# A hybrid decoder layer: another order in which heads, gates and parts of x are admitted

## The chip, the cores and the metric

The kernel runs on one core of one Trainium2 chip. The metric is the device time of one launch in microseconds (us). A time that is given without more is the median of several runs of the same program. The profile is that of one single execution.

## What is computed

One layer of a decoder over a prompt of 2,048 tokens and 8 sample tokens. The input is normalised and multiplied by one wide matrix `w_in` (1,024 x 11,280). Its columns feed two branches and two merge gates: a gated DeltaNet with 8 heads (GDN, a recurrence over chunks of tokens), and a dilated window attention with 3 groups of 4 heads.

```python
def mixer_inputs(x, g_pre, w_in):
    xn = rms_norm(x, g_pre)
    proj = jnp.einsum('bld,de->ble', xn, w_in)
...
    def step(S, inp):
        u_c, w_c, qk_c, qd_c, kd_c, gl_c = inp
        v_new = u_c - jnp.einsum('bhcd,bhde->bhce', w_c, S)
        o_c = jnp.einsum('bhcd,bhde->bhce', qd_c, S) + jnp.einsum('bhce,bhef->bhcf', qk_c, v_new)
        S = S * gl_c[..., None, None] + jnp.einsum('bhcd,bhce->bhde', kd_c, v_new)
        return S, o_c
...
def merge_residual(x, p_a, p_b, gate_a, gate_b, w_out, g_post):
    h = jax.nn.sigmoid(gate_a) * p_a + jax.nn.sigmoid(gate_b) * p_b
    out = jnp.einsum('bld,de->ble', h, w_out)
    return x + rms_norm(out, g_post)
```

The sample tokens go through the same layer, with a GDN state and key and value caches that are read from memory. All states are outputs too.

## The kernel before

**Two halves.** The prompt is worked on in two halves of 1,024 tokens (`hf` 0 and 1); the sample tokens ride with the first. For each half the input projection runs over 128-column tiles of `w_in`, two tiles at a time. After both halves a final phase multiplies by `w_proj_a`, `w_proj_b` and `w_out` in four token groups.

**Products (`main`).** A pair of tiles is one call of `step`. It saves multiplications on half of the contraction by sums of inputs and weights. Its products read `xs1k` to `xs7k` and `xp4s` to `xp7s` (x, transposed) against `wh` and `wl` (the weights, split into a high and a low part); in a row of TensorE a product has one of these names, and `bank0` to `bank3` as its target. The order inside a pair is fixed: product 1, product 7, product 6, product 2 and so on. Product 6 (`xs6k`) accumulates onto a copy of product 1 in `bank1`, so it waits (`at_b`) until `bank1` has been emptied by the `sink` of the pair before.

**Pages and tokens.** A `sink` copies a finished tile from its PSUM bank into a page `pg` (17 pages of SBUF, 4 KB a partition and a little more) and then frees the bank. The first of a tile's sinks waits for `t.admit`, the tile's token, and then for a free page. Tokens (17, as many as pages) are given out by `admitter` strictly in the order of the list `admits`; a request that can't be met holds up all that stand behind it. A task hands its tokens back when it is done with its pages. So when tokens run out, the sinks stop, the banks stay full, and `main` stops before a product.

**Side tasks.** On `bank4` to `bank7` run the heads. `gdn` of a head does a convolution, transposes, a triangular inverse, and then a serial loop over 8 chunks, each a chain through three engines: kT times `st` on TensorE, `rr` on VectorE (L311), U times `rr` on TensorE, a copy to `ww` (ScalarE L280 or VectorE L355), kd times `ww` on TensorE, `st` on VectorE (L311). TensorE rows that read `st`, `rr` or `ww` are this loop. One head is in the loop at a time. `attn` is the attention of a group and head, `combine` joins the groups, `sample_gdn` and `sample_attn` are the sample tokens, `prep` loads, normalises and transposes x for a half and forms the sums of its rows on VectorE (L316 on pages).

**What sets the order.** All of these are generators. `Scheduler.run` plays them at build time with a table of costs and latencies and writes each engine's instruction list in the order in which it finds them ready, ties going by priority. On the chip each engine runs its list in that order, and a wait at the head of the list holds all behind it.

**`ORDER`.** Two strings (L2171 and L2172), one for each half, are read a character at a time. `G` adds the three tiles of the next GDN head (and claims 4 more tokens for its work), `Z` that head's gate tile, `a` the q, k and v tiles of one attention group (each fourth `a` is a combine gate), `g` a merge gate tile. `x` and `y` claim 5 and 4 tokens for the preparation of the second half's x, `S`, `T` and `C` claim 4, 3 and 1 for the sample GDN, the sample attention and the convolution state. The string thus sets both the order of the tiles in the projection (`p["work"]`) and the order of `admits`. Lines of the trace: all matmuls are L251, transposes L267, ScalarE L280, VectorE L299, L301, L311, L316 and L355, loads and stores L400.

Of the kernel before, what the change touches and what calls it, by code (L numbers as in the profile page):

```python
# [453 lines left out]
def build(nc, tc, ctx, I, O):  # L454
# [1702 lines left out]
    def conv_state():  # L2157
# [10 lines left out]
    plan, admits = [], []  # L2168


    ORDER = ("GZaaGaZaGaagZGgaZagGZaagGagagZGagaZGaZagggggggxgyg",  # L2171
             "gGgZggaagGaZSagGaZaGaZgaggGaagTZGaZaCggGaaZgGZaggag")  # L2172
    for hf in range(2):
        tiles = []

# [45 lines left out]

        for what in ORDER[hf]:
            if what in "GZag":
# [108 lines left out]
def trace(nc, arrays):  # L2332
    from contextlib import ExitStack

    ins = {n: nc.dram_tensor(f"in_{n}", a.shape, mybir.dt.from_np(a.dtype), kind="ExternalInput").ap()
           for n, a in arrays.items()}
    outs = [nc.dram_tensor(f"out_{i}", s, F32, kind="ExternalOutput").ap() for i, s in enumerate(_OUTS)]
    with tile.TileContext(nc) as tc, ExitStack() as ctx:
        return build(nc, tc, ctx, ins, outs)
# [13 lines left out]
```

## Time and profile before

| | |
|---|---|
| median of 3 runs | 3048.79 us (3048.49 to 3049.93) |
| the profiled execution | 3050.04 us |
| its span in the trace | 3048.2 us |
| TensorE busy | 3010.0 us, 99% of the span |
| TensorE weight loads busy | 2692.0 us, 88% |
| VectorE, ScalarE, GpSimd busy | 72%, 40%, 5% |
| mean granted TensorE clock | 0.996 |

The profiled execution lies 1.25 us above the median, and 1.84 us of its time are outside the span. Times inside the trace count from the start of the span. TensorE is called PE in the rows, its weight loads PEld, VectorE DVE, ScalarE ACT. A granted clock of 1.00 is 2.4 GHz, one of 0.5 is 1.2 GHz. The ends of matmuls are modelled in the trace and overlap the next matmul, so how long a matmul holds the engine is read from start to start.

### The profile page before, as it was taken

How to read it: one execution, taken by the hardware profiler on the slowest of the kernel's cores; microseconds unless marked ns; L12 is line 12 of the kernel's file. 1: busy time of each engine (PE TensorE's matmuls, PEld its weight loads, DVE VectorE, ACT ScalarE, POOL GpSimd, SP SyncE). 2: the span in 40 equal slices, each digit the busy share in tenths (PEclk: the TensorE clock that was granted, in tenths of full speed). 3: DMA queues.
4: the chain of work that ended last, by engine and by line, in shares of the span. 5: the costliest groups of instructions: out<-in, count | busy, mean ns of one | idle time of the engine just before them, and what ended most of it. 6: DMA issues, size and time to landing. Idle time of an engine off the chain costs nothing.

```text
span 3048.2 us, 55885 instructions
## 1 busy us (share of the span) xinstructions
PE 3010.0 (99%) x20879; PEld 2692.0 (88%) x20879; DVE 2199.2 (72%) x5978; ACT 1212.9 (40%) x3444; POOL 141.1 (5%) x239
## 2 busy tenths in 40 slices
PE   7999999999999999999999999999999999999999
PEld 7999999999999999978887888888888888897887
DVE  6777767786778686767586868597988486666765
ACT  5545444344435443433442534343434343313121
POOL 1000000000000000000000000000000000000000
PEclk9999999999999999999999999999999999999999
DMA  4323242332233325332244332336452236565463
GB/s 125 94 73 89 58 112 71 99 85 83 70 98 89 89 79 147 110 85 81 73 121 124 88 88 80 105 96 186 137 158 86 76 100 180 176 204 197 149 226 117
DMA packets 468760, 343.46 MB, mean 113 GB/s; under 512 B 88745, under 2 KB 411825, under 8 KB 468480
## 3 DMA queue, kind: packets, MB, share of 16 engines
q1 hardware_dynamic: 468488, 339.89, 38.1%
q8 instruction: 164, 2.69, 0.4%
q14 instruction: 108, 0.88, 0.1%
HBM read 261.40 MB, written 80.97 MB: 112 GB/s over the span
## 4 chain that ended last, share of the span: by engine, by line
PE 94%; DVE 3%; DMA 2%; ACT 1%; issue 0%; SPq 0%; POOL 0%; DVEq 0%; POOLq 0%; ACTq 0%
PE bank L251 89%; PE bank L267 5%; DVE pg L311 1%; DMA wr<-in_w_in 0%; DVE wl L316 0%; DVE pg L316 0%; SPq L400 0%; DMA pg<-in_cache_v_w 0%; DMA pg<-in_x_prompt 0%; DMA pg<-in_state_gdn 0%; DMA pg<-gate 0%; ACT L280 0%; DMA ghh<-in_g_head_norm 0%; DVE wh L355 0%; DVE junk L311 0%
## 5 line engine op out<-in xcount | busy, mean ns | idle before, releaser
L280 ACT ACTIVATE pg<-bank 128x256 f32<-128x256 f32 (+7 forms) x741 | 331.8, 460 | 759.4 <-PE bank L251 690.0
L316 DVE TENSOR_TENSOR wl<-wr,wh 128x512 fp32r<-128x512 f32 x595 | 383.5, 647 | 21.3 <-ACT wh L280 3.3
L355 DVE CAST wh<-wr 128x512 fp32r<-128x512 f32 (+1 forms) x384 | 153.0, 399 | 206.9 <-PE bank L251 184.0
L251 PE MATMUL bank<-xp7s,wh 128*128 128x512 f32 (+3 forms) x1196 | 302.1, 328 | 0.0
L251 PE MATMUL bank<-xp6s,wh 128*128 128x512 f32 (+3 forms) x1132 | 290.1, 330 | 0.0
L251 PE MATMUL bank<-xp5s,wh 128*128 128x256 f32 (+3 forms) x1100 | 276.3, 327 | 0.0
L280 ACT ACTIVATE wh<-wr 128x512 fp32r<-128x512 f32 (+1 forms) x213 | 129.8, 611 | 351.9 <-PE bank L251 292.1
L251 PE MATMUL bank<-xp4s,wh 128*128 128x260 f32 (+2 forms) x1068 | 267.5, 326 | 1.6 <-DVE xp4s L311 1.6
L316 DVE TENSOR_TENSOR bank<-bank,etmp 128x256 f32<-128x256 f32 (+2 forms) x260 | 134.9, 519 | 129.4 <-PE bank L251 126.3
L251 PEld LDWEIGHTS bank<-xp7s,wh 128*128 128x128 f32 x1196 | 198.4, 188 | 17.5 <-issue 1.7
L251 PEld LDWEIGHTS bank<-xp6s,wh 128*128 128x128 f32 (+1 forms) x1132 | 189.2, 188 | 17.2 <-issue 0.8
L251 PEld LDWEIGHTS bank<-xp5s,wh 128*128 128x128 f32 (+1 forms) x1100 | 183.0, 188 | 14.7 <-issue 0.2
L251 PE MATMUL bank<-xp7s,wl 128*128 128x512 f32 (+3 forms) x592 | 195.0, 329 | 0.0
L251 PEld LDWEIGHTS bank<-xp4s,wh 128*128 128x128 f32 x1068 | 176.1, 188 | 14.9 <-DVE xp4s L311 1.8
L280 ACT ACTIVATE prob<-bank 128x512 f32<-128x512 f32 (+4 forms) x224 | 105.2, 482 | 208.7 <-PE bank L251 120.8
L311 DVE SCALAR_TENSOR_TENSOR pg<-pg,convw,pg 128x1024 f32<-128x1024 f32 x144 | 183.9, 1277 | 2.8 <-ACT pg L280 1.3
L251 PE MATMUL bank<-xp6s,wl 128*128 128x512 f32 (+2 forms) x560 | 184.9, 330 | 0.0
L251 PE MATMUL bank<-xp5s,wl 128*128 128x512 f32 (+2 forms) x544 | 178.5, 328 | 0.0
L251 PE MATMUL bank<-xs1k,wh 128*128 128x512 f32 (+4 forms) x708 | 177.8, 334 | 0.0
L251 PE MATMUL bank<-xp4s,wl 128*128 128x256 f32 (+2 forms) x528 | 172.5, 327 | 0.0
L251 PE MATMUL bank<-xs6k,wh 128*128 128x512 f32 (+3 forms) x680 | 171.3, 334 | 0.0
L251 PE MATMUL bank<-xs7k,wh 128*128 128x512 f32 (+3 forms) x680 | 169.9, 333 | 0.0
(302 smaller groups left out, 7474.8 us busy)
## 6 DMA issues: line engine op xcount, KB each, us to landing
wr<-in_w_in SPq DMA_DIRECT2D x176, 512.0 KB
pg<-in_x_prompt SPq DMA_DIRECT2D x32, 512.0 KB
pg<-grow SPq DMA_DIRECT2D x32, 512.0 KB
wr<-in_w_proj_a SPq DMA_DIRECT2D x32, 512.0 KB
wr<-in_w_out SPq DMA_DIRECT2D x32, 512.0 KB
pg<-og SPq DMA_DIRECT2D x24, 520.0 KB
pg<-gate SPq DMA_DIRECT2D x24, 512.0 KB
out<-pg SPq DMA_DIRECT2D x20, 512.0 KB
```

The source lines that it names most:

```text
L251: nc.tensor.matmul(out, lhsT, rhs, start=start, stop=stop, skip_group_check=shared)
L267: nc.tensor.transpose(out, in_, ident[:k, :k])
L280: return ("act", c, lambda: nc.scalar.activation(out, in_, func, **kw))
L311: lambda: nc.vector.scalar_tensor_tensor(out, in0, scalar, in1, op0=op0, op1=op1, **kw))],
L316: return ("dve", self._vcost(out, in0, in1), lambda: nc.vector.tensor_tensor(out, in0, in1, op=op))
L355: alts.append(("dve", self._vcost(out, in_, fast=True), lambda: nc.vector.tensor_copy(out, in_)))
```

## The change

The two strings are replaced by two others with the same number of each letter. In the first, `x` stands in place 36 and not 46. In the second, `S` stands in place 2 and not 13, `T` in place 24 and not 31, `C` in place 29 and not 36.

```diff
@@ -2168,8 +2168,8 @@
     plan, admits = [], []
 
 
-    ORDER = ("GZaaGaZaGaagZGgaZagGZaagGagagZGagaZGaZagggggggxgyg",
-             "gGgZggaagGaZSagGaZaGaZgaggGaagTZGaZaCggGaaZgGZaggag")
+    ORDER = ("GZaaGZaaGaggaGZaaZGagagGZgagagZGaZaGxaggaZgggggygg",
+             "GSagZgagGaagZGgaaGZagZgTggagCGgaagGZgZaaGaZgaGgaaZg")
     for hf in range(2):
         tiles = []
 
```

The multiset of tiles, tasks and instructions stays: TensorE has 18,281 matmuls in both programs, the DMAs are 1,409 in both; 10 copies change from VectorE to ScalarE. But the place of nearly everything after TensorE's row 1,280 (of some 13,500 rows, equal neighbours joined) moves. Three places are shown.

**The second GDN head of the first half, TensorE.** Its loop reads `rr` with `pg13` in both programs. Before, one stretch of its loop reads (from row 2,083):

```order
L251 MATMUL bank4_69<-st1_146,pg15_110 128x128
L251 MATMUL bank6_71<-st1_146,pg11_106 128x128
L251 MATMUL bank4_69<-rr_143,pg13_108 128x128
L251 MATMUL bank4_69<-ww_144,pg7_102 128x128
L251 MATMUL bank6_71<-ww_144,pg4_99 128x128
L251 MATMUL bank4_69<-st1_146,pg15_110 128x128
L251 MATMUL bank6_71<-st1_146,pg11_106 128x128
L251 MATMUL bank1_66<-xs6k0_83,wh4_122 128x260 x2
```

After, the middle of the same head's loop reads (from row 2,074):

```order
L251 MATMUL bank5_70<-rr_143,pg13_108 128x128
L251 MATMUL bank0_65<-xp5s0_89,wl3_121 128x260
L251 MATMUL bank0_65<-xp6s0_91,wh3_120 128x260
L251 MATMUL bank0_65<-xp6s1_92,wh3_120 128x260
L251 MATMUL bank0_65<-xp6s0_91,wl3_121 128x260
L251 MATMUL bank0_65<-xp7s0_93,wh3_120 128x260
L251 MATMUL bank0_65<-xp7s1_94,wh3_120 128x260
L251 MATMUL bank5_70<-ww_144,pg7_102 128x128
L251 MATMUL bank0_65<-xp7s0_93,wl3_121 128x260
L251 MATMUL bank1_66<-xs5k0_81,wh4_122 128x260
L251 MATMUL bank6_71<-ww_144,pg4_99 128x128
```

Before, eleven loop rows (the seven shown and four ahead of them) follow each other with no product between; after, products on `bank0` and `bank1` stand between any two steps of the loop.

**The sixth GDN head of the second half, TensorE.** Its loop reads `rr` with `pg15` before and with `pg7` after. Before (from row 11,102; the next product, `xs6k`, is row 11,140):

```order
L251 MATMUL bank2_67<-xs7k1_86,wl3_121 128x512
L251 MATMUL bank6_71<-ww_144,pg1_96 128x128
L251 MATMUL bank4_69<-ww_144,pg3_98 128x128
L251 MATMUL bank6_71<-st1_146,pg14_109 128x128
L251 MATMUL bank4_69<-st1_146,pg8_103 128x128
L251 MATMUL bank6_71<-rr_143,pg15_110 128x128
L251 MATMUL bank6_71<-ww_144,pg1_96 128x128
L251 MATMUL bank4_69<-ww_144,pg3_98 128x128
L251 MATMUL bank6_71<-st1_146,pg14_109 128x128
L251 MATMUL bank5_70<-cst_128,pg7_102 128x1
```

After (from row 11,181):

```order
L251 MATMUL bank7_72<-ww_144,pg10_105 128x128
L251 MATMUL bank1_66<-xs3k0_77,wl3_121 128x512
L251 MATMUL bank5_70<-ww_144,pg2_97 128x128
L251 MATMUL bank1_66<-xs3k1_78,wh3_120 128x512 x2
L251 MATMUL bank7_72<-st1_146,pg15_110 128x128
L251 MATMUL bank1_66<-xs3k1_78,wl3_121 128x512
L251 MATMUL bank5_70<-st1_146,pg13_108 128x128
L267 MATMUL bank6_71<-cst_128,prob1_177 128x128 x4
L251 MATMUL bank7_72<-rr_143,pg7_102 128x128
L251 MATMUL bank1_66<-xp4s0_87,wh5_124 128x512
```

Before, 37 rows of loop, transposes and sample attention stand between two products; after, products lie between the steps here too. The longest stretch of TensorE rows without a product is elsewhere in after, early in the second half. It begins at row 8,280 and is made of an inverse (32x32 and 64x64), attention (128x128 with `prob1` and `pg13`) and the sample GDN (128x2), and ends with row 8,301; in its middle stands (from row 8,286):

```order
L251 MATMUL bank6_71<-pg3_98,pg13_108 128x128
L251 MATMUL bank6_71<-pg0_95,pg13_108 128x128
L251 MATMUL bank6_71<-pg3_98,pg13_108 128x128
L251 MATMUL bank4_69<-prob2_178,pg10_105 32x32 x8
L251 MATMUL bank4_69<-pg10_105,prob2_178 32x32 x16
L251 MATMUL bank7_72<-pg6_101,pg7_102 128x2 x7
L251 MATMUL bank6_71<-prob0_176,pg10_105 64x64 x8
L267 MATMUL bank5_70<-cst_128,prob1_177 128x128 x4
L251 MATMUL bank4_69<-pg3_98,pg13_108 128x128 x4
L251 MATMUL bank6_71<-pg10_105,prob2_178 64x64 x8
```

Its steps belong to four tasks that alternate, where before's longest stretch is mostly one loop.

**VectorE at the boundary of the halves.** The rows that end the preparation of the second half's x, from its last scaling (`xp7s`) on. Before:

```order
L311 SCALAR_TENSOR_TENSOR xp7s1_94<-bank4_69,gpre_129,xp7s0_93 128x512
L316 TENSOR_TENSOR pg3_98<-pg3_98,pg7_102 128x256
L316 TENSOR_TENSOR pg7_102<-pg10_105,pg9_104 128x256
L355 CAST wh5_124<-wr0_112 128x512
L316 TENSOR_TENSOR pg9_104<-pg10_105,pg7_102 128x256
L316 TENSOR_TENSOR wl5_125<-wr0_112,wh5_124 128x512
L316 TENSOR_TENSOR pg9_104<-pg9_104,pg7_102 128x256
L316 TENSOR_TENSOR pg7_102<-pg16_111,pg2_97 128x256
L316 TENSOR_TENSOR pg2_97<-pg16_111,pg7_102 128x256
L316 TENSOR_TENSOR pg2_97<-pg2_97,pg7_102 128x256
L316 TENSOR_TENSOR wr1_113<-wr1_113 128x32
L316 TENSOR_TENSOR xs7k0_85<-bank7_72,xs7k0_85 128x512
```

After (the rows behind `xp7s`):

```order
L316 TENSOR_TENSOR pg9_104<-pg9_104,pg0_95 128x256
L316 TENSOR_TENSOR pg0_95<-pg12_107,pg13_108 128x256
L311 SCALAR_TENSOR_TENSOR pg2_97<-bank6_71,pg2_97 128x512
L316 TENSOR_TENSOR pg13_108<-pg12_107,pg0_95 128x256
L316 TENSOR_TENSOR wl5_125<-wr0_112,wh5_124 128x512
L316 TENSOR_TENSOR pg13_108<-pg13_108,pg0_95 128x256
L316 TENSOR_TENSOR pg0_95<-pg10_105,pg15_110 128x256
L316 TENSOR_TENSOR pg15_110<-pg10_105,pg0_95 128x256
L316 TENSOR_TENSOR pg15_110<-pg15_110,pg0_95 128x256
L316 TENSOR_TENSOR pg0_95<-pg16_111,pg5_100 128x256
L316 TENSOR_TENSOR pg5_100<-pg16_111,pg0_95 128x256
L316 TENSOR_TENSOR pg5_100<-pg5_100,pg0_95 128x256
```

After, three more sums of pages and one scaling of a gate tile (`pg2` from `bank6`) stand between `xp7s` and the last sum of pages, and a cast is gone.

## Rows read from the trace of the kernel before

**Rows 1.** The page: span and busy time of each engine
```profile
span 3048.2 us, 55885 instructions
...
PE 3010.0 (99%) x20879; PEld 2692.0 (88%) x20879; DVE 2199.2 (72%) x5978; ACT 1212.9 (40%) x3444; POOL 141.1 (5%) x239
```

**Rows 2.** The page: the chain that ended last, share of the span by line
```profile
PE bank L251 89%; PE bank L267 5%; DVE pg L311 1%; DMA wr<-in_w_in 0%; DVE wl L316 0%; DVE pg L316 0%; SPq L400 0%; DMA pg<-in_cache_v_w 0%; DMA pg<-in_x_prompt 0%; DMA pg<-in_state_gdn 0%; DMA pg<-gate 0%; ACT L280 0%; DMA ghh<-in_g_head_norm 0%; DVE wh L355 0%; DVE junk L311 0%
```

**Rows 3.** Stretches: length; busy PE, PEld, DVE, ACT, POOL; granted clock, DMA share, GB/s
```profile
0.00:35.00 35.00, 18.66 (x125) 16.81 (x126) 25.17 (x78) 21.27 (x54) 11.55 (x30) 1.00 0.68 200
362.50:369.65 7.15, 4.54 (x24) 3.12 (x22) 6.33 (x19) 5.82 (x24) 1.09 (x1) 0.95 0.01 2
369.65:373.00 3.35, 3.35 (x19) 3.35 (x19) 2.12 (x7) 0.52 (x2) 0.00 (x0) 0.61 0.00 0
1280.50:1284.00 3.50, 3.50 (x18) 3.50 (x19) 2.50 (x5) 2.21 (x4) 0.00 (x0) 0.55 0.60 168
1624.90:1628.50 3.60, 3.60 (x10) 2.71 (x9) 1.85 (x8) 0.60 (x1) 0.00 (x0) 0.53 0.71 199
2302.40:2322.90 20.50, 17.13 (x86) 14.10 (x84) 13.40 (x35) 8.36 (x34) 1.01 (x1) 0.75 0.48 132
```

**Rows 4.** Timeline of TensorE, first loop: start, us, line, operands, count [idle before <-releaser]
```profile
357.48 0.83 PE L251 MATMUL bank<-pg,pg 128*128 128x128 f32 x6
358.15 0.39 PE L251 MATMUL bank<-ww,pg 128*128 128x128 f32 x2
...
362.54 0.38 PE L251 MATMUL bank<-st,pg 128*128 128x128 f32 x2
...
363.93 0.71 PE L251 MATMUL bank<-ww,pg 128*128 128x128 f32 x4 [0.43 <-ACT ww L280]
364.86 0.71 PE L251 MATMUL bank<-st,pg 128*128 128x128 f32 x4 [0.22 <-DVE st L311]
...
368.64 1.03 PE L251 MATMUL bank<-st,pg 128*128 128x128 f32 x4 [1.10 <-DVE st L311]
369.65 0.80 PE L251 MATMUL bank<-xs6k,wh 128*128 128x260 f32 x2
```

**Rows 5.** Timeline of VectorE before TensorE goes on at 369.65
```profile
367.10 1.23 DVE L316 TENSOR_TENSOR pg<-pg,pg 128x1024 f32<-128x1024 f32 x1
```

**Rows 6.** Timeline of TensorE, the second loop
```profile
2302.43 0.47 PE L251 MATMUL bank<-xs7k,wl 128*128 128x512 f32 x1
...
2322.93 0.72 PE L251 MATMUL bank<-xs6k,wh 128*128 128x512 f32 x2
```

**Rows 7.** Waits of TensorE over the span: us in total, times, longest us
```profile
PE bank L251 <- DVE st L311: 2.7, 6, 1.1
PE bank L251 <- DVE rr L311: 2.4, 4, 0.9
...
PE bank L251 <- ACT ww L280: 1.4, 4, 0.4
```

**Rows 8.** Timeline of TensorE at the boundary of the halves
```profile
1278.77 0.33 PE L267 MATMUL bank<-cst,pg 128*128 128x128 f32 x1 [1.68 <-DVE pg L316]
1280.51 3.59 PE L267 MATMUL bank<-cst,pg 128*128 128x128 f32 x17 [1.40 <-DVE pg L316]
```

**Rows 9.** Timeline of VectorE at the boundary of the halves
```profile
1274.98 0.74 DVE L311 SCALAR_TENSOR_TENSOR xp5s<-bank,gpre,xp5s 128x512 fp32r<-128x512 f32 x1
...
1279.24 1.54 DVE L316 TENSOR_TENSOR pg<-pg,pg 128x256 f32<-128x256 f32 x4
```

**Rows 10.** The chain in order of time: start us, us, what
```profile
1206.94 8.56 DMA pg<-in_x_prompt
...
1615.05 7.49 DMA pg<-in_state_gdn
```

**Rows 11.** Timeline of TensorE behind those two transfers
```profile
1221.77 0.46 PE L251 MATMUL bank<-rr,pg 128*128 128x128 f32 x2 [0.93 <-DVE rr L311]
...
1622.58 1.95 PE L251 MATMUL bank<-pg,pg 128*128 128x2 f32 x16 [0.68 <-DMA pg<-in_state_gdn]
```

## The prediction

> **What bounds the kernel now.** I read the page first. TensorE is busy 3010.0 us of a span of 3048.2 [rows 1], and 89% of the chain that ended last is TensorE on L251, products and heads [rows 2]. The multiset of matmuls does not change, so the order can win back only what TensorE loses: 38.2 us of idle, and what it loses where its clock stands at 1.2 GHz. Of the idle, 35.00 - 18.66 = 16.3 us lie in the first 35 us [rows 3], ahead of the first row that the change moves, and stay.
>
> Then I looked for places where the rest is lost, from start to start, with 0.11 us for an f32 matmul record of 128 columns (six take 358.15 - 357.48 = 0.67 us) [rows 4]. Two stretches stand out. In both the GDN loop runs on TensorE with no product between its steps, because `main` has stopped before product 6 (`xs6k`) for want of `bank1`; the sink that should empty it waits for a page. In the first, VectorE ends the big sum of another head at 368.3 [rows 5], a page comes free, and the product starts at 369.65 [rows 4]. A loop step that is not covered costs TensorE the way to another engine and back: two `ww` steps with 4 records start at 363.93, the next `st` at 364.86, so 0.93 us for 0.44 us of work, of which two records (0.22) stand behind the result: a result needs about 0.93 - 0.44 + 0.22 = 0.7 us of other TensorE work behind it, or TensorE waits [rows 4].
>
> - **First loop.** From 362.54 to 369.65 are 7.11 us with 22 records (the window counts two that began earlier), 2.4 us of work: 4.7 lost [rows 3, 4]. Then the clock is granted at 0.61 for 3.35 us, which loses 0.39 x 3.35 = 1.3. Together 6.0.
> - **Second loop.** From 2302.4 to 2322.9 are 20.5 us [rows 3, 6]. Behind the last product (about 0.2 us) stand 82 records, 9.0 us of work (of the window's 86, the others began earlier or are the product). Lost: 20.5 - 9.0 - 0.2 = 11.3 us. The granted clock is 0.75 over the stretch, so 0.25 x 20.5 = 5.1 of the 11.3 are clock, and 6.2 waiting.
>
> The waits of TensorE say the same from the other side: most of the waits for `st` (2.7 us), `rr` (2.4) and `ww` (1.4) lie in these two stretches [rows 7].
>
> **The change part by part.** Nothing is added or removed, so every term is a loss that goes, stays or comes.
>
> *Loops without products go: -6.0 and -11.3.* In the order of after, products stand between the loop steps of both heads, and I counted for all 16 heads how much TensorE work stands between a step and the result it reads. Before, five `ww` steps have none and many others 0.22 to 0.44 us, all in the two stretches; after, none has under 0.66 us. Against a need of 0.7 that is enough to lose at most some hundredths a step. If the clock fell in those places for another reason, 1.3 + 5.1 = 6.4 of the gain would not come.
>
> *The boundary of the halves: +1.2.* TensorE waits 1.68 and 1.40 us there for sums of pages on VectorE, and its clock then falls to 0.55 [rows 3, 8]. After, three more sums stand behind the last split of weights, 3 x 1.54 / 4 = 1.2 us [rows 9]; the extra scaling (0.74 by its likeness in before [rows 9]) stands ahead of that split, which waits for the last product anyway. Bounds: +0.4, if the first transposes start sooner, and +1.9 with the scaling. What stands behind this on VectorE is the first `xs7k`, for which the products of the second half wait, so the term is on the path. The fall of the clock stays as it is.
>
> *Parts of x earlier: -1.1.* `x` moves up ten places. Before, VectorE stood at the head of its list for a part of x that landed at 1215.5, `rr` came late, and TensorE waited [rows 10, 11]; counted from start to start this lost 1.1 us. After, over 40 us of TensorE work stand between each such load's release and the work on it. Bounds: -1.1 and 0.
>
> *Sample GDN earlier: +1.7.* `S` moves the eight loads of sample states (7.49 us each [rows 10]) from the middle of the second half to its beginning. One of them was late before: TensorE waited 0.8 us at 1622.58 [rows 11], and its clock then fell to 0.53 for 3.6 us, another 1.7 [rows 3], so 2.5 us for one late load. Counting the TensorE work between the row that frees the page and the row that reads the state, three of eight loads had 8.4 us or less before, and one was late; after, it is five of eight (the least 6.5). At one in three I expect 1.67 late loads, 0.67 more than now: 0.67 x 2.5 = 1.7. Bounds: none late, -2.5; all five late, +10. The store queue is the same SyncE queue in both programs, and the loads of weights keep over 13 us of cover, so I price nothing else there.
>
> *The other waits: 0.* Of the 38.2 us of idle, 16.3 are the first 35 us, 2.6 and 3.4 the two loops, 3.1 the boundary, 0.7 and 0.9 the late state and x [rows 1, 3, 8, 11]. The remaining 11 us are small waits of under 1.6 us, spread over the span. They meet another order by chance; the thin places (0.7 to 2 us of cover) are about as many after as before, so I keep them, within 4 us either way. The final phase starts with about the same cover and is not touched.
>
> Sum: -6.0 - 11.3 + 1.2 - 1.1 + 1.7 + 0 = -15.5 us. On the profiled execution 3050.04 - 15.5 = 3034.5; that lay 1.25 above the median, so the median becomes 3048.79 - 15.5 = **3033.3 us**.
>
> **The rivals.**
>
> *A, the loss moves.* Tokens and pages are as few as before. If all five thin state loads come late (+10 in place of +1.7) and the clock falls once more at the longer boundary (another 1.7), the time is 3033.3 + 8.3 + 1.7 = 3043.3. For it: the five covers are close to the load's 7.49 us, and the loads now follow the boundary, where x and weights are loaded too. Against it: a load with 6.8 us of cover was in time before.
> The Trainium skill (Perfetto Trace Analysis, section "Optimization Strategy") speaks against the change more strongly: a gap that repeats on the engine that should be saturated can mean that there isn't enough SBUF or PSUM for the next tile, so buffers or tile sizes are what to change. The trace agrees on the cause (TensorE goes on at 369.65 when a page comes free), and by the page's rule, with still 17 pages, the whole 17.3 us would come back elsewhere: 3033.3 + 17.3 = 3050.6. The order speaks against that, since no uncovered loop is left in it.
>
> *B, slower: other work without products.* After has four stretches of side work without a product, 9.8, 5.7, 4.8 and 4.4 us of TensorE work, 24.7 in all, the longest early in the second half. If these lose as the second loop did (11.3 us for 9.0 of work, 1.25 each), they cost 24.7 x 1.25 = 31 us, and the time is 3033.3 + 31 = 3064. It decides at the need of 0.7 us: in before's stretch the steps had 0 to 0.4 us between them. In the four they have 0.9 and more, since several tasks alternate there, and before had stretches of 5.5 and 4.0 us of such work that show no wait among the largest. So I hold it for unlikely; VectorE, with operations of 1.2 us at the head of its list, would have to be late at nearly every step.
>
> *C, the clock falls all the same* in the two places: 3033.3 + 6.4 = 3039.7. For it: the transposes and small matmuls of the heads stay. Against it: both falls come behind waits.
>
> *D, nothing changes*, 3048.8: the order differs from row 1,280 on, so this can only be chance.
>
> **How the numbers follow.** The forecast, within its bounds, has 75%, C 8%, A 11% (with the whole loss returning, 2 of these), B 5%, D 1%. A measurement of this kernel tells 0.2% (6.1 us) from no change: faster is under 3042.7, slower over 3054.9. The forecast and C are faster, and A in one case of 11: 84%. A's others and D are the same: 11%. B is slower: 5%. The low end takes no late state (-4.2 against the sum) and a little luck in the small waits: 3028. The high end takes in A: 3043.5. B, D and some of the forecast's own tails are left out.
>
> **What would show it.** In the profile of after: no wait for `ww` among the largest waits and `st` and `rr` together under 2 us; no stretch of over 1 us at a low clock in the first half behind the first 35 us; the two waits at the boundary together about 4.3 us in place of 3.1; one or two waits of TensorE for the sample states early in the second half; TensorE busy about the same 3005 to 3010 us in a span shorter by 15. It is wrong if a stretch with the clock at 0.75 or less over more than 5 us stands early in the second half (B), or if `main` again stops for a page at a place where the order shows products (then covers counted from the order are no guide).

## The result

The changed kernel takes 3033.85 us (median of 4 runs, 3033.24 to 3034.75) where the kernel before takes 3049.11 (median of 4, 3048.49 to 3049.93). The ratio is 0.995, with a 95% interval of 0.9933 to 0.9967: 15.3 us or 0.5% faster. The prediction was 3033.3 us, with a range of 3028.0 to 3043.5. The profiled execution is the fastest of the four, 3033.24 us, and that of before, 3050.04, lies above its four, so the two profiles differ by 16.8 us.

The page of the changed kernel, which answers to [rows 1]:

```profile
span 3031.4 us, 55905 instructions
...
PE 3002.5 (99%) x20879; PEld 2689.0 (89%) x20879; DVE 2198.7 (73%) x5969; ACT 1216.3 (40%) x3453; POOL 138.0 (5%) x239
```

TensorE's busy time falls by only 7.5 us, its idle time from 38.2 to 28.9. The rest of the gain is in the busy time: matmuls that ran at half the clock count as busy. The stretches (columns as in [rows 3]) around the places of the prediction:

```profile
0.00:35.00 35.00, 20.02 (x122) 18.37 (x123) 24.91 (x77) 21.71 (x54) 10.99 (x30) 0.95 0.70 198
355.00:380.00 25.00, 25.00 (x222) 24.93 (x220) 20.74 (x62) 10.07 (x37) 1.14 (x1) 1.00 0.17 46
1262.00:1271.50 9.50, 6.72 (x49) 5.81 (x47) 9.43 (x22) 4.92 (x11) 0.43 (x1) 1.00 0.40 153
1271.50:1274.90 3.40, 3.37 (x16) 3.28 (x17) 1.81 (x5) 2.09 (x4) 0.02 (x1) 0.50 1.05 261
1285.10:1288.50 3.40, 3.40 (x10) 2.58 (x9) 2.42 (x7) 0.62 (x4) 0.00 (x0) 0.51 0.06 14
1322.70:1326.10 3.40, 3.40 (x13) 2.50 (x11) 2.82 (x14) 0.81 (x5) 0.00 (x0) 0.50 0.00 0
1483.10:1486.50 3.40, 3.40 (x20) 3.17 (x20) 0.54 (x3) 1.26 (x3) 0.00 (x0) 0.50 0.00 0
2291.00:2321.00 30.00, 30.00 (x194) 26.69 (x193) 23.86 (x59) 13.26 (x44) 1.52 (x2) 1.00 0.30 74
```

In the stretches where the second GDN head of the first half and the sixth of the second half now run their loops (357 to 380 and 2292 to 2320 us), TensorE is busy for the whole time at the full clock. Before, the same two heads had 0.95, 0.61 and 0.75 [rows 3]. The boundary of the halves (1262 to 1275) looks as before: 2.8 us idle, then the clock at 0.50. New are three stretches of 3.4 us at half the clock without any idle time, at 1285, 1323 and 1483 us.

Some of the waits of TensorE over the span (us in total, times, longest us):

```profile
PE bank L267 <- DVE pg L316: 2.8, 3, 1.5
...
PE bank L251 <- DVE st L311: 0.7, 2, 0.5
```

Against [rows 7], `st` has gone from 2.7 us to 0.7, and `rr`, `ww` and the sample state are no longer in the list.

To size each place I took, for every matmul, the time to the next one's start, less the median of the same three kinds of neighbours in that trace. The sum of these excesses, kept apart for matmuls at half the clock, is the loss:

| place | before: waits + clock, us | after | forecast of the change | measured |
|---|---|---|---|---|
| first 35 us | 9.7 + 0 | 8.6 + 1.4 | 0 | +0.3 |
| first loop | 4.2 + 1.8 | 0 | -6.0 | -6.0 |
| second loop | 5.0 + 6.0 | 0 | -11.3 | -11.0 |
| boundary of the halves | 3.5 + 1.5 | 3.4 + 1.6 | +1.2 | 0 |
| part of x, then `rr` late | 1.2 + 0 | 0 | -1.1 | -1.2 |
| sample GDN, early second half | 0.9 + 1.6 | 0 + 3.5 | +1.7 | +1.0 |
| all else | 8.8 + 0 | 8.6 + 0 | 0 | -0.2 |
| sum | 44.2 | 27.1 | -15.5 | -17.1 |

The spans differ by 16.8.

### The profile page after: what moved, and what is told of

Its sections match the earlier page's. It is cut to its first block, busy times and chain, and to the rows that moved or that the text cites. A ratio compares the mean times of both kernels' runs of the same rounds, so it can differ in the third digit from the quotient of the medians.

```text
span 3031.4 us, 55905 instructions
## 1 busy us (share of the span) xinstructions
PE 3002.5 (99%) x20879; PEld 2689.0 (89%) x20879; DVE 2198.7 (73%) x5969; ACT 1216.3 (40%) x3453; POOL 138.0 (5%) x239
## 4 chain that ended last, share of the span: by engine, by line
PE 93%; DVE 4%; DMA 1%; issue 0%; ACT 0%; SPq 0%; POOL 0%; DVEq 0%; POOLq 0%; ACTq 0%
PE bank L251 88%; PE bank L267 5%; DVE pg L311 1%; DVE wl L316 1%; DMA pg<-ya_d 1%; DMA wr<-in_w_in 0%; DVE pg L316 0%; DVE lane_x L316 0%; SPq L400 0%; DVE lane_t L316 0%; DVE wh L355 0%; DVE junk L311 0%; DMA pg<-og 0%; ACT L280 0%; DMA pg<-sq_d 0%
## 5 line engine op out<-in xcount | busy, mean ns | idle before, releaser
L280 ACT ACTIVATE pg<-bank 128x256 f32<-128x256 f32 (+8 forms) x739 | 333.5, 462 | 761.7 <-PE bank L251 682.1
L251 PE MATMUL bank<-xp6s,wh 128*128 128x512 f32 (+3 forms) x1196 | 300.5, 328 | 0.0
L251 PE MATMUL bank<-xp7s,wh 128*128 128x256 f32 (+3 forms) x1164 | 291.4, 326 | 0.0
L251 PEld LDWEIGHTS bank<-xp6s,wh 128*128 128x128 f32 x1196 | 197.6, 188 | 16.2 <-issue 0.8
L251 PEld LDWEIGHTS bank<-xp7s,wh 128*128 128x128 f32 x1164 | 192.2, 188 | 15.4 <-issue 1.0
L251 PE MATMUL bank<-xp6s,wl 128*128 128x512 f32 (+3 forms) x592 | 193.7, 327 | 0.0
L251 PE MATMUL bank<-xp7s,wl 128*128 128x256 f32 (+3 forms) x576 | 188.6, 327 | 0.0
L251 PEld LDWEIGHTS bank<-xp4s,wh 128*128 128x128 f32 x1068 | 176.2, 188 | 13.2
L251 PE MATMUL bank<-xs2k,wh 128*128 128x512 f32 (+4 forms) x708 | 179.2, 335 | 0.2 <-DVE xs2k L316 0.2
L280 ACT ACTIVATE prob<-bank 128x512 f32<-128x512 f32 (+3 forms) x215 | 102.0, 487 | 170.5 <-PE bank L251 110.0
```

The source lines that it names most:

```text
L251: nc.tensor.matmul(out, lhsT, rhs, start=start, stop=stop, skip_group_check=shared)
L280: return ("act", c, lambda: nc.scalar.activation(out, in_, func, **kw))
```

## Experiments

In the three sets of runs that follow, the kernel before took 3050.7, 3050.8 and 3049.9 us (medians) and scattered more than at first (3045.6 to 3057.6). So every run is compared with the runs of before on the same chip in its own set. The changed kernel itself, run once more in the second set, stands at 0.9947 there.

**One string at a time.** First only the first string:

```diff
-    ORDER = ("GZaaGaZaGaagZGgaZagGZaagGagagZGagaZGaZagggggggxgyg",
+    ORDER = ("GZaaGZaaGaggaGZaaZGagagGZgagagZGaZaGxaggaZgggggygg",
              "gGgZggaagGaZSagGaZaGaZgaggGaagTZGaZaCggGaaZgGZaggag")
```

> Only the first string is changed, the second is that of before. Theory (each loop stretch without products carries its own loss, and the halves don't depend on each other): in the order of this kernel the uncovered loop of the first half is gone and that of the second half stands as before, so the gain is the 6.0 us of the first loop and the 1.1 us of the late part of x: about 3041.7 us by the median of before, 3048.8; no TensorE wait for ww near 360 us, the waits and the low clock near 2300 us as in before. Rival (the loss only moves, and it takes both strings to win): 3046 to 3050.

Measured: 3040.99 us (ten runs, 3038.50 to 3048.44), ratio 0.9973 (0.9962 to 0.9983), so 8.2 us faster. Stretches of its trace:

```profile
355.00:380.00 25.00, 25.00 (x224) 24.93 (x223) 20.52 (x61) 10.08 (x37) 1.14 (x1) 1.00 0.18 46
2290.00:2311.00 21.00, 17.44 (x86) 14.38 (x85) 14.21 (x38) 7.77 (x33) 1.01 (x1) 0.76 0.45 129
```

The first loop's stretch has no idle time, the second loop's stands as before: 3.6 us idle and a clock of 0.76 (0.75 in [rows 3]). The theory said 7, which lies in the interval (5.2 to 11.6). (The profiled execution gained 11.5; in it the sample state was in time as well, which before it was not.)

Then only the second string:

```diff
     ORDER = ("GZaaGaZaGaagZGgaZagGZaagGagagZGagaZGaZagggggggxgyg",
-             "gGgZggaagGaZSagGaZaGaZgaggGaagTZGaZaCggGaaZgGZaggag")
+             "GSagZgagGaagZGgaaGZagZgTggagCGgaagGZgZaaGaZgaGgaaZg")
```

> Only the second string is changed, the first is that of before. Theory: the first loop keeps its loss, the second loop's 11.3 us go, and the sample GDN at the beginning of the second half costs what it does in the changed kernel (falls of the clock near 1285, 1322 and 1483 us, 1.0 more than the one late state of before): 3048.8 - 11.3 + 1.0 = 3038.5 us. The two single gains add up to that of both strings within 1.5 us. Rival (they don't add, since a string moves what follows it): a sum that is off by over 4 us.

Measured: 3042.48 us (ten runs, 3039.06 to 3046.00), ratio 0.9975 (0.9965 to 0.9984), 7.6 us faster (4.9 to 10.7) where 10.3 were expected. Stretches:

```profile
361.00:368.00 7.00, 5.56 (x38) 4.50 (x36) 5.15 (x18) 4.52 (x19) 0.05 (x1) 0.93 0.01 2
368.00:374.00 6.00, 5.46 (x24) 5.03 (x25) 4.57 (x12) 2.10 (x7) 1.04 (x1) 0.52 0.00 0
2301.00:2322.00 21.00, 21.00 (x132) 18.32 (x131) 17.73 (x40) 10.03 (x32) 1.01 (x1) 1.00 0.38 94
```

The first loop has its waits and its low clock (0.93 and 0.52 here, a fall of 6.8 us in place of 3.4), the second loop's stretch is full. The two single gains are 0.27 and 0.25%, both strings together gave 0.50 to 0.53%: they add up. The falls of the clock in the second half did not come where I expected them: in the profiled execution they were at 1446, 1490 and 2132 us, with none at the boundary, although the second string is the same and TensorE's rows from the boundary on are those of the changed kernel, name by name. The waits at the boundary are those of before (1.68 and 1.40 us), and the fall at 1446 stands behind a sample state that came 0.24 us late.

**One page less.** All else as in the changed kernel:

```diff
-    NPAGE = 17
+    NPAGE = 16
```

> The changed kernel with 16 pages and tokens in place of 17. Theory (the stops of the products are a shortage of pages, and their cost can be counted from the order): the order of this kernel has loop steps without enough work between them again, near 225 us and near 333 us into the work and some near 2550, with 20 us more missing work than in the changed kernel (24.8 against 5.3, the need of each step less the TensorE work between); in before the two loops had 15.0 us of it and lost 17.0 with the clock, so here +22 us: 3056 us. Rival (pages don't matter once the order is good): 3034 us, no change from the changed kernel.

Measured: 3065.6 us, ratio 1.0049 (1.0032 to 1.0066), so 30 us slower than the changed kernel. TensorE's waits for `ww` and `rr` are back:

```profile
PE bank L251 <- ACT ww L280: 4.3, 10, 0.5
...
PE bank L251 <- DVE rr L311: 2.0, 6, 0.9
```

and so are stretches with idle time and a low clock, at the places that the order named. Of the three, those near 250 and 370 us of the trace:

```profile
248.00:258.00 10.00, 6.56 (x38) 4.99 (x38) 8.70 (x25) 4.97 (x20) 1.16 (x1) 0.95 0.01 2
258.00:262.00 4.00, 4.00 (x26) 4.00 (x26) 2.75 (x8) 0.28 (x1) 0.00 (x0) 0.70 0.00 0
370.00:380.00 10.00, 9.13 (x33) 7.07 (x32) 7.59 (x22) 3.17 (x14) 1.14 (x1) 0.50 0.01 2
```

So it is the supply of pages that stops the products, and where it runs short can be read from the order. The size was wrong: the run lost 30 us, not 22. By the count of the table, waits are 15.6 us more than in the changed kernel and the half clock 13.2 more: an uncovered stretch pays a second time in the clock. By the same count the three places (the third is near 2650 us) lost 7, 12 and 7 us, so some 26 for the 20 us of missing work; the rest is mostly longer or added falls of the clock at the boundary and in the second half.

**x earlier still, and `S` later.** Against the changed kernel `x` moves up four places and `S` moves from index 1 to 7:

```diff
-    ORDER = ("GZaaGZaaGaggaGZaaZGagagGZgagagZGaZaGxaggaZgggggygg",
-             "GSagZgagGaagZGgaaGZagZgTggagCGgaagGZgZaaGaZgaGgaaZg")
+    ORDER = ("GZaaGZaaGaggaGZaaZGagagGZgagagZGxaZaGaggaZgggggygg",
+             "GagZgagSGaagZGgaaGZagZgTggagCGgaagGZgZaaGaZgaGgaaZg")
```

> The changed kernel with x four places earlier still in the first string (index 32), y at 47 and S at index 7 of the second. x's five tokens are then taken while the last heads of the first half need theirs. Theory (tokens decide, and the cost is what the order lacks): about 1024 us into the work a stretch of 16.3 us of TensorE rows without a product, with 19 loop steps short of work, 16.3 us in all; with the clock 1.13 to 1.46 as much, 18 to 24 us, of which 2 to 3 come back since the sample GDN meets less: 3050 to 3057 us where the changed kernel takes 3034. Rival (an earlier x is better or harmless, since its loads have more time): 3034 or less.

Measured: 3065.1 us (one run), 31 us above the changed kernel on the same chip. The stretch is there:

```profile
1053.00:1080.00 27.00, 21.80 (x197) 19.19 (x196) 11.61 (x28) 9.73 (x31) 0.00 (x0) 0.71 0.13 31
1080.00:1092.00 12.00, 11.11 (x42) 8.88 (x42) 5.92 (x23) 4.46 (x18) 2.81 (x3) 0.52 0.00 0
```

In 27 us TensorE is idle for 5.2 and has a mean clock of 0.71, and the 12 us behind it run at 0.52. From 1064 to 1091 us the clock stood at half without a break, which cost 15.1 us by the count of the table. By the same count the whole stretch, 1053 to 1103 us, lost 21 us (6 of waits, 15 of clock), within the 18 to 24 that the theory gave it. What failed in the theory is that the sample GDN would meet less: about 9 of the 31 us lie between 1400 and 1560 us, where two sample states came 1.5 and 0.5 us late and the clock stood at half for 13.7 us from 1501 us on. So the 31 us are not those of `x` alone. The stretch itself shows the mechanism that rival B of the prediction feared: side work whose steps have too little between them is dear.

**Two other orders near the changed one.** First `y` two places earlier and `S` at index 5:

```diff
-    ORDER = ("GZaaGZaaGaggaGZaaZGagagGZgagagZGaZaGxaggaZgggggygg",
-             "GSagZgagGaagZGgaaGZagZgTggagCGgaagGZgZaaGaZgaGgaaZg")
+    ORDER = ("GZaaGZaaGaggaGZaaZGagagGZgagagZGaZaGxaggaZggggyggg",
+             "GagZgSagGaagZGgaaGZagZgTggagCGgaagGZgZaaGaZgaGgaaZg")
```

> The changed kernel with y two places earlier in the first string and S at index 5 in place of 1 in the second. Theory: by the order no loop step is short of work, the boundary of the halves has 2.6 us of missing work in place of 4.8, so that 2 us go there; the sample GDN still runs early in the second half with small matmuls between products, so one to three falls of the clock stay (1.0 to 1.3 us each): 3030 to 3033 us. Rival (the boundary's wait is set by something else than the order of its sums): 3034 us, with waits of 3.4 us at the boundary as in the changed kernel.

Measured: 3031.54 us, ratio 0.9937 (0.9921 to 0.9953). The number is in the range that the theory gave, but its reason is not there: the waits at the boundary were 3.6 us, as in before and in the changed kernel, so the rival is right about the boundary. What went are the falls of the clock near 1285, 1323 and 1483 us. What came is a wait of 2.0 us at 1970 us, with a fall of the clock behind it. The timelines of VectorE and, below, of TensorE there:

```profile
1968.76 0.29 DVE L311 SCALAR_TENSOR_TENSOR junk<-pg 128x128 bf16<-128x128 f32 x1 [1.72 <-DMA pg<-sq_d]
```

```profile
1970.72 0.49 PE L251 MATMUL bank<-rr,pg 128*128 128x128 f32 x2 [2.00 <-DVE rr L311]
```

VectorE stood at the head of its list for a load of the sample GDN (`sq_d`) that was late by 1.7 us, and the `rr` of a GDN loop stood behind it.

Then `S` back at the index that it had before, all else as changed:

```diff
-             "GSagZgagGaagZGgaaGZagZgTggagCGgaagGZgZaaGaZgaGgaaZg")
+             "GagZgagGaagZSGgaaGZagZgTggagCGgaagGZgZaaGaZgaGgaaZg")
```

> The changed kernel with S back at index 12 of the second string, as in before; all else as changed. Theory (sample GDN early costs falls of the clock near 1286, 1323 and 1484 us, 3.5 us together, and nothing else): the falls near 1286 and 1323 are gone, the one at 1484 may stay or move; against it stand two loop steps short of work near 1640 us (2.7 us by the order) and the chance of one late state (2.5): 3032 to 3036 us, no clear difference from 3034. Rival (S early is what saves the order of the second half): 3040 us or more.

Measured: 3043.16 us, ratio 0.998 (0.997 to 0.999): 9 to 10 us slower than the changed kernel, so the theory falls and the rival stands. A sample state is late (timeline of TensorE), and later the clock falls for 10.2 us (stretches):

```profile
1722.97 2.13 PE L251 MATMUL bank<-pg,pg 128*128 128x2 f32 x16 [2.24 <-DMA pg<-in_state_gdn]
```

```profile
1718.00:1724.00 6.00, 3.76 (x22) 2.94 (x20) 1.12 (x2) 1.46 (x2) 0.00 (x0) 1.00 1.09 243
1786.00:1796.00 10.00, 10.00 (x42) 7.65 (x41) 3.42 (x6) 3.14 (x5) 0.19 (x1) 0.50 0.69 184
```

Besides there are 3.0 us of waits in a loop near 1651 us, which the order named, a late `rr` at 1227 us (0.95) as in before, and a fall of 6.8 us at the boundary in place of 3.4. The late state waits 2.2 us while the DMA engines are busy for the whole stretch at 243 GB/s. The sample GDN early is thus worth about 9 us in this order, though its own account against before comes to a loss of 1.0: it has to be somewhere, and later it met a loop short of work and a late state. Whether scarce pages or full DMA queues matter more is not told apart by this run.

**The changed kernel once more.** No edit.

> The changed kernel once more, unchanged, for two questions. The clock: its first profile had falls to 0.5 near 1271, 1285, 1323 and 1483 us, the last three behind no wait of TensorE; the kernel with the second string alone has the same order there and had falls near 1446 and 1490 instead. Theory (the falls behind small side matmuls are partly chance): in this execution some of the falls near 1285, 1323 and 1483 are gone or elsewhere, the waits at 1268 to 1272 us are again 3.4 us. Rival (they belong to the order): the same places again. The time: on a chip where before takes 3050.7, 3035 to 3036 us.

Measured: 3034.04 us (3033.83 to 3034.79), ratio 0.9947. The falls:

```profile
1272.40:1275.80 3.40, 3.26 (x18) 2.87 (x16) 1.62 (x4) 2.39 (x4) 0.00 (x0) 0.51 1.04 243
1286.10:1289.50 3.40, 3.40 (x11) 2.65 (x9) 2.29 (x7) 0.46 (x2) 0.00 (x0) 0.50 0.06 16
1323.60:1327.00 3.40, 3.40 (x12) 2.50 (x12) 2.82 (x14) 0.94 (x5) 0.00 (x0) 0.51 0.00 0
1484.10:1487.50 3.40, 3.40 (x21) 3.18 (x20) 0.78 (x4) 1.46 (x3) 0.00 (x0) 0.50 0.00 0
```

They are the same four, each about 1.0 us later in the span (as is all that follows the first 40 us). The rival is right: they belong to this program. That in one execution with another first string they stood elsewhere, with the same rows on TensorE, suggests that they hang on more than TensorE's own order; on what is not shown.

**The sums at the boundary on GpSimd.** The sums of the pages of x, so far only VectorE's, may go to whichever of VectorE and GpSimd ends first by the scheduler's table (4 lines, one shown):

```diff
-            yield K.tt(s2, s1, a11, OP.subtract)
+            yield K.tt_any(s2, s1, a11, OP.subtract)
```

> The changed kernel, where the sums of the pages of x (L316 on pages, 16 for each half) may go to GpSimd too; 11 of the second half's 16 do, and 8 of the first half's. Theory (the 3.4 us of waits at the boundary of the halves are VectorE's total work in the last 15 us, so the place of a sum among its rows doesn't matter, only how many there are): with 11 sums of 0.34 us less on VectorE the two waits fall from 3.4 us to under 1.5, and if the clock doesn't fall there either, another 1.6 us go: 2 to 3.5 us faster than the changed kernel on the same chip. Rival (the sums on GpSimd take over a microsecond each, one after the other, and become the last thing TensorE waits for): no gain, or up to 4 us slower, with TensorE waiting for POOL at the boundary.

Measured: 3026.04 us (3023.90 to 3027.36), ratio 0.9919 (0.9905 to 0.9934); 8.0 us faster than the changed kernel on the same chip. TensorE at the boundary:

```profile
1267.10 1.91 PE L267 MATMUL bank<-cst,pg 128*128 128x128 f32 x16
1268.76 0.36 PE L251 MATMUL bank<-xp7s,wl 128*128 128x260 f32 x1
1269.26 2.57 PE L267 MATMUL bank<-cst,pg 128*128 128x128 f32 x16
1271.58 0.48 PE L251 MATMUL bank<-xs7k,wh 128*128 128x512 f32 x1
```

Where the changed kernel has waits of 0.54, 1.47 and 0.80, no row here has one that the profile shows; from start to start 0.9 us are lost. Of two stretches, the boundary and the only low clock of the second half,

```profile
1260.00:1271.50 11.50, 11.36 (x87) 10.25 (x86) 10.78 (x21) 6.75 (x15) 3.96 (x5) 1.00 0.32 122
1473.70:1480.50 6.80, 6.80 (x38) 5.88 (x38) 2.03 (x7) 1.95 (x6) 0.00 (x0) 0.50 0.55 157
```

the first has the full clock. So the waits were VectorE's total work there, as the theory has it. It gave little more than half of the gain, though: 4.4 us at the boundary (2.5 of the waits and the 1.8 of the clock) of the 7.4 by which the times from the first to the last matmul differ in the two traces on this chip. Falls that cost 3.7 us at three places have turned into one of 3.1 at 1474, small waits are 0.8 less, and 1.6 us are in the medians of TensorE's own work, which I have not followed.

With the same edit in the second half only:

```diff
-            yield K.tt(s2, s1, a11, OP.subtract)
+            yield (K.tt_any if hf else K.tt)(s2, s1, a11, OP.subtract)
```

> The changed kernel with only the second half's sums of pages open to GpSimd; those of the first half stay on VectorE. Theory (the gain of 8.0 us lies at the boundary and behind it, since the first 35 us were the same with the sums): 3026 us, as with both. Rival (the first half's sums carry 2 us or more of it): 3028 to 3031 us.

Measured: 3025.30 us (3023.51 to 3027.39), ratio 0.9917 (0.9903 to 0.9932): as with both halves, so the gain comes from the second half's sums. It is 0.8% under the kernel before, and not told apart from the run with both halves.

With the edit in the kernel before:

> The kernel before, with its own two strings, where the sums of x's pages may go to GpSimd (L320). Theory (the wait at the boundary of the halves is VectorE's work there and has nothing to do with the order of admission): the waits of 3.5 us at 1277 to 1280 us and the fall of the clock behind them (1.5) go, the two loops near 363 and 2302 us keep their 17 us: 4 to 5 us faster than before; with the 15 us of the order this makes up the 23 to 25 us between before and the changed kernel with these sums. Rival (part of the 8 us that the sums gave the changed kernel came from another order behind the boundary): 7 us or more, or under 2.

Measured: 3045.33 us, ratio 0.9989 (0.9979 to 0.9999), 3.4 us faster (0.3 to 6.4). Stretches of its trace:

```profile
361.00:374.00 13.00, 10.90 (x58) 9.57 (x57) 10.72 (x31) 6.70 (x26) 1.08 (x1) 0.74 0.00 1
1274.00:1282.00 8.00, 6.81 (x53) 5.69 (x52) 7.90 (x16) 6.76 (x13) 0.00 (x0) 1.00 0.43 141
2295.00:2317.00 22.00, 18.56 (x93) 15.45 (x92) 15.14 (x40) 8.81 (x34) 1.01 (x1) 0.77 0.46 123
```

The two loops keep their losses (0.74 and 0.77 of the clock), and the boundary has its full clock; 2.0 us of waits are left there, not 0.9. The theory's 4 to 5 us lie in the interval. But 3.4 and the order's 15 to 16 make 19 us, and both together gave 25: some 6 us appear only in the new order, in part as the falls that went. With 0.3 to 6.4 us as the interval of the 3.4, part of the 6 may be noise; the rest stays open.

With the edit in the kernel with `y` and `S` moved:

> The kernel with y two places earlier and S at index 5, with the sums of x's pages open to GpSimd too (12 of the second half's 16 go there). Theory: the gains add, the boundary's waits go from 3.6 us to under 1.5 and the sample GDN keeps its place: 2 to 3.5 us less than without, 3028 to 3030 us on a chip where before takes 3050.7. Rival: as in the run before, GpSimd becomes what TensorE waits for, 3031 us or more.

Measured: 3032.73 us (3028.99 to 3036.58), ratio 0.9945 (0.9928 to 0.9961), against 0.9937 without the edit. The boundary's waits went from 3.6 to 1.9 us and the clock doesn't fall there, but the wait behind `sq_d` is still 2.0, and the four runs lie 7.6 us apart. Nothing follows but that the gains don't simply add.

## Why the prediction was right

**The two loops** were the forecast, and they are nearly all of the result: -17.3 expected, -17.0 measured. Both steps behind it held. In the two loops no step makes TensorE wait, and over the whole span the loops' waits are two for `st`, 0.7 us in all, with none for `rr` and `ww`. The longer of the two, 0.49 us at 2641.85, stands behind a single product, where the prediction's count of the order had no step with under 0.66 us of work. With the waits the low clock went too, so rival C, by which the clock falls in the same places, is out. The runs with one string show that the two losses are separate.

**The boundary, +1.2, was 0.** The step that failed is "that split waits for the last product anyway". In the changed kernel:

```profile
1267.67 0.28 PE L251 MATMUL bank<-xp7s,wl 128*128 128x260 f32 x1
...
1268.60 0.33 PE L267 MATMUL bank<-cst,pg 128*128 128x128 f32 x1 [0.54 <-DVE pg L316]
1270.40 0.33 PE L267 MATMUL bank<-cst,pg 128*128 128x128 f32 x1 [1.47 <-DVE pg L316]
1271.53 3.69 PE L267 MATMUL bank<-cst,pg 128*128 128x128 f32 x17 [0.80 <-DVE pg L316]
```

```profile
1268.53 0.69 DVE L316 TENSOR_TENSOR wl<-wr,wh 128x512 fp32r<-128x512 f32 x1
1269.14 2.67 DVE L316 TENSOR_TENSOR pg<-pg,pg 128x256 f32<-128x256 f32 x7
```

The split (`wl`) starts 0.86 us after the last product does. In the kernel before, TensorE's last product and VectorE's split stand so:

```profile
1276.49 0.29 PE L251 MATMUL bank<-xp7s,wl 128*128 128x260 f32 x1
...
1278.64 0.68 DVE L316 TENSOR_TENSOR wl<-wr,wh 128x512 fp32r<-128x512 f32 x1
```

There it started 2.15 us after. VectorE, not the product, had set its start: it is busy for 9.43 of the 9.5 us ahead of 1271.5 in the changed kernel, and 8.1 of 8.5 ahead of the same place before. The three sums that now stand behind the split stood ahead of `xp7s` before, and the split starts about that much sooner. What counts there is how much VectorE has to do; the runs with sums on GpSimd show it. The order counted for little in the three orders seen: the run with `y` earlier had one that looked better, and its waits were the same.

**x, -1.1, was -1.2**: the late part of x, the late `rr` behind it and the wait are gone.

**Sample GDN, +1.7, was +1.0, for another reason.** None of the eight states came late, so rival A (3043.3) did not come about; the load with 6.5 us of cover was in time, while before one of three with 8.4 us or less was late, and with `S` back one was late by 2.2. TensorE work between issue and use is thus a poor measure for a load; what else the DMA queues carry would have to be in it. In its place came something that the prediction did not have: three falls of the clock where TensorE does not wait, 1.0 to 1.3 us each. (The 0.8 us of the prediction for the late state of before is not what its row shows, 0.68; from start to start it is the 0.9 of the table, so the price of 2.5 stands.)

**Rival B (3064)** was the right danger and rightly held unlikely for this order: its longest stretch without a product ran from about 1476 to 1488 us, without a wait, and cost one fall of the clock, 1.3 us and not 12. Where stretches hold steps that are short of work, as with one page less or with x earlier, they cost about 1.3 us for each us of missing work (26 for 20, 21 for 16.3), near the rate of 1.25 that the rival took, though it counted that for each us of side work.

**The Trainium skill's rule** (Perfetto Trace Analysis, "Optimization Strategy"), that a repeating gap can mean too little SBUF or PSUM for the next tile, is borne out as to the cause by the run with 16 pages. What the prediction drew from it for the rival, that the loss comes back elsewhere as long as there are 17 pages, is not: with the same 17 pages another order lost 17 us less.

**Signs and luck.** Of the signs that the prediction named, the waits of the loops and the clock of the first half came. Three did not: the two waits at the boundary are not 4.3 us but 2.8 in three, no sample state was late, and TensorE is busy for 3002.5 us where 3005 to 3010 were named, since time at half the clock, which counts as busy, went too. That the median meets the forecast within 0.6 us is partly luck: the boundary came out 1.2 us and the sample GDN 0.7 us better than priced, and the two profiles differ by 16.8 us where the medians differ by 15.3.

## What to carry to other kernels

When a pool of buffers feeds several tasks in a fixed order, look for stretches in which the bound engine runs one serial chain alone, and count for each step how much other work stands between it and the result it needs: that count found both losses and, in other orders, their return, though not the falls of the clock elsewhere. Price such a stretch above the missing work (1.1 to 1.3 times here: 17.0 us for 15.0 before, 26 for 20 with a page less, 21 for 16.3 with x earlier), since the low clock is part of it. At the boundary, a wait in which another engine was busy nearly throughout got shorter when work was taken off that engine, and not when its work was put in another order.

## What the runs showed of the hardware

**The clock fell where TensorE did not wait.** At 1322.7 and 1483.1 us of the changed kernel, in both executions with a profile, the granted clock went from 1.00 (2.4 GHz) to 0.50 (1.2 GHz) for 3.4 us. Ahead of it stood matmuls of the sample GDN with 2 columns each and others with 64 (timelines of TensorE ahead of the first and of the second fall):

```profile
1319.05 1.84 PE L251 MATMUL bank<-pg,pg 128*128 128x2 f32 x16
...
1321.62 0.88 PE L251 MATMUL bank<-pg,pg 128*128 128x64 f32 x6 [0.38 <-DVE pg L316]
```

```profile
1480.31 1.72 PE L251 MATMUL bank<-pg,pg 128*128 128x2 f32 x14
1481.96 1.14 PE L251 MATMUL bank<-prob,pg 64*64 64x64 f32 x16
```

The fall at 1322.7 also follows a wait of 0.4 us, that at 1483.1 none. Each cost 1.0 to 1.3 us. What in this work makes the clock fall is not shown.

**VectorE and GpSimd slow each other, by what VectorE reads.** In the run with sums on GpSimd, rows of the timelines of VectorE and, below, of GpSimd:

```profile
39.20 1.29 DVE L316 TENSOR_TENSOR xs5k<-bank,xs5k 128x512 fp32r<-128x512 f32 x2
...
1261.77 1.22 DVE L316 TENSOR_TENSOR wl<-wr,wh 128x512 fp32r<-128x512 f32 x1
...
1265.43 0.69 DVE L316 TENSOR_TENSOR wl<-wr,wh 128x512 fp32r<-128x512 f32 x1
```

```profile
39.29 3.64 POOL L320 TENSOR_TENSOR pg<-pg,pg 128x256 f32<-128x256 f32 x5 [2.55 <-PE bank L267]
...
1260.82 3.67 POOL L320 TENSOR_TENSOR pg<-pg,pg 128x256 f32<-128x256 f32 x4 [2.30 <-PE bank L251]
```

The same split of a weight tile, which reads both operands from SBUF, takes VectorE 1.22 us while GpSimd runs four sums, and 0.69 when GpSimd has ended; the four sums take GpSimd 3.67 / 4 = 0.92 us each. At 39 us, where VectorE reads one of its operands from a PSUM bank, neither is slowed: five sums take GpSimd 3.64 / 5 = 0.73 us each, and VectorE's two operations take 1.29 us, against 1.28 in the changed kernel, where GpSimd has no sums. The Trainium skill (SBUF — State Buffer, "SBUF: two separate sides") states that the two share a pair of ports as an exclusive lock, which a VectorE operation with two inputs in SBUF takes too; the longer times agree, and so does the row without them. That it is a lock and not a shared rate is not worked out here. The sums still paid off, since 11 of 16 left VectorE.
